# Two splits of the PSUM banks, the decays of a group made ahead, and an eighth tile for sample states

## The chip, the cores and the metric

The kernel runs on one NeuronCore of a Trainium2 chip. The metric is the device time of one execution in microseconds; the time given is the median of several runs. A profile is one execution more, recorded by the hardware profiler, and has a time of its own. The core has five engines that work side by side, each through its own queue of instructions: TensorE (PE; its loading of the stationary operand is shown as PEld), VectorE (DVE), ScalarE (ACT), GpSimd (POOL) and SyncE (SP), which here only issues transfers. TensorE writes to PSUM, eight banks of 128 x 512 fp32 numbers.

## The reference

One inference step of a model with two layers, for a prompt of 256 tokens and eight sample streams of 16 tokens (384 tokens together), width 1024, all in fp32:

```python
for i in range(DEPTH):                       # DEPTH = 2
    h = rms_norm(x, norm_mix[i])
    if i % 2 == 0:                           # layer 0: short conv and attention
        out, k, v, lf, sc = even_mixer(h, ...)
    else:                                    # layer 1: Mamba-2 SSD (SSM)
        out, cs, ss = odd_mixer(h, ...)
    x = x + out
    f, fs = conv_ffn(rms_norm(x, norm_ffn[i]), ...)
    x = x + f
```

`even_mixer` projects to a gated short convolution (512 channels) and to eight attention heads with a forget gate, joins the two and multiplies by `w_out`. `odd_mixer` projects to z, to the convolved x, B and C, and to dt, and runs a state-space scan over 32 heads in four groups:

```python
cum = jnp.cumsum(dtc * a, axis=2)
seg = cum[:, :, :, None] - cum[:, :, None, :]
decay = jnp.exp(jnp.where(tri[:, :, None, None], seg, -jnp.inf))
mix = cb[..., None] * decay * dtc[:, :, None]
y_intra = jnp.einsum('bcqsgr,bcsgrp->bcqgrp', mix, xc)
```

To it comes the part of the state that a sequence brings along (a state of 64 x 128 per head for each sample stream), and the state after the step is an output. `conv_ffn` multiplies by `w_up` (2 x 2816 columns), convolves one half, gates, and multiplies by `w_down`.

## The kernel before

All 384 tokens stand in the free dimension of the tiles, features in the partitions. Weights come as 219 tiles of 128 x 1024 (`raw`), loaded by SP in the order of their use. Each is split into two fp32r tiles, `wh` by ACT (L364) and `wl` by DVE (L365); the activations are split likewise (`Hh`, `Hl`), and a product is three matmuls (`three`, L404): high x high, high x low, low x high (profile lines L405 to L407). `wraw` and `wsp` have three buffers each. `fm_group` makes 128 output features for all tokens in one bank; `tm_group` makes three banks, one for each 128 tokens, with 512 features.

The stages in order of time: q, k and v (`tm_group`, three banks each, to about 78 us); the attention, with the short convolution's projections (`short_conv`: banks gc, gu, gb) beside it; the output projection `op`; the first FFN (`fa`, `fg`, then `fd`, to 470 us); the SSM layer (to about 788 us: `xbc` in `conv4`, z, and `op` in `add_out`); the second FFN.

Engine queues are laid out when the program is built. The framework takes the instructions in the order of the Python program as their priority, and puts on each engine the one of highest priority that can run by its own estimate of durations and with tiles that are free; `tc.high_priority()` moves weights ahead. Where the program calls `fill(n)`, some steps of a generator with projections are put between the steps of the scan. On the chip each queue runs in the order laid out. A pool's `bufs` says how many tiles of a tag exist; an instruction that needs one more waits for a release. Matmul results live in two PSUM pools, opened once for the whole kernel: `mm`, three banks, for the projections (`pmm`), and `aux`, five banks, for all else (`paux`).

In the SSM layer `channels(g)` makes a group's x, B, C (`xt`, `CB`, `Bt`, `Bm`), and `scan` runs over b = 0, 1 (two blocks of 128 prompt tokens) and b = 2 (the samples). In blocks 0 and 1 it makes the decays of eight heads in two halves: `td`/`tdr` on DVE (L1044), a matmul `sg` with cum as both operands (L1047), Relu and Exp on ACT into `dec` (tag `td`, two buffers; L1053, L1054), and `mix` from `dec` and `CB` on DVE (L1055). In block 2 it goes over the eight sample states in two fours (`par`): load `h0` (SP, L1079), matmul `yi` (L1082), matmul `hn` (L1089), a product on POOL and a sum on DVE in place, store `o_hs` from ACT's queue (L1096). The prompt's state after block 1, `S1` (L1110), takes a tile of the same tag `h0`, with seven buffers, and is stored as `o_hp` from POOL's queue (L1113).

Of the kernel before, what the change touches and what calls it, by code (L numbers as in the profile page):

```python
# [18 lines left out]
P = 128  # L19
# [64 lines left out]
def _pack(x):  # L84

    x = {k: np.asarray(v) for k, v in x.items()}
    a = {}
    tok = np.concatenate([x["x_prompt"][0], x["x_sample"].reshape(NB * LB, -1)], 0)
    a["x"] = tok.T.reshape(KT, P, NT)

    blocks = []

    def fm(w, cols, kts=None):

        n = w.shape[0] // P
        for c in cols:
            for kt in (range(n) if kts is None else kts):
                blocks.append(w[kt * P:(kt + 1) * P, c:c + P])

    def tm(w, c):  # L100

        for kt in range(w.shape[0] // P):
            blocks.append(w[kt * P:(kt + 1) * P, c:c + 512])

    wi, wo = x["w_in_even"][0], x["w_out_even"][0]
    tm(wi, 1536), tm(wi, 2048), tm(wi, 2560)
    for i in range(4):
        fm(wi, (512 + P * i, 1024 + P * i, P * i))
    first = [P * m for m in range(3)]
    fm(wo, first, range(0, 4))  # L110
    fm(wo, first, range(4, 8))
    fm(wo, range(3 * P, 1024, P))

    def ffn(layer):
        wu, wd = x["w_up"][layer], x["w_down"][layer]
        for j in range(NF):
            fm(wu, (P * j, P * (NF + j)))
        fm(wd, range(0, 1024, P))

    ffn(0)  # L120
    wi, wo = x["w_in_odd"][0], x["w_out_odd"][0]

    def chan(g):
        fm(wi, (4096 + P * g, 4608 + P * g))
        fm(wi, range(2048 + 512 * g, 2560 + 512 * g, P))

    def out(g):
        for c in (0, 512):
            for kt in range(4 * g, 4 * g + 4):
                blocks.append(wo[kt * P:(kt + 1) * P, c:c + 512])  # L130

    chan(0)
    for g in range(4):
        if g < 3:
            chan(g + 1)
        tm(wi, 512 * g)
        if g:
            out(g - 1)
    out(3)
    ffn(1)  # L140
    w = np.concatenate(blocks, 1)
    a["w"] = w.reshape(P, -1, RC).transpose(1, 0, 2)

    def small(w):

        t = np.zeros((P, KT, 32), np.float32)
        t[:, :, :w.shape[1]] = w.reshape(KT, P, -1).transpose(1, 0, 2)
        return t.reshape(P, -1)

    a["wsm"] = np.concatenate([small(x["w_in_even"][0][:, 3072:]), small(x["w_in_odd"][0][:, 5120:])], 1)  # L150

    prm = np.zeros((P, NPRM), np.float32)

    def put(name, arr, off=0):
        o = COL[name] + off
        prm[:, o:o + arr.shape[1]] = arr

    for l in range(2):
        put("g_mix", _cols(x["norm_mix"][l]), 8 * l)
        put("g_ffn", _cols(x["norm_ffn"][l]), 8 * l)  # L160
        for t in range(3):
            put("cvf", _cols(x["ffn_conv_w"][l, t]), (3 * l + t) * NF)
        put("cvfb", _cols(x["ffn_conv_b"][l]), l * NF)
    for t in range(3):
        put("cva", _cols(x["conv_a_w"][0, t]), 4 * t)
    for t in range(4):
        put("cvs", _cols(x["ssm_conv_w"][0, t]), 24 * t)
    put("sng", _cols(x["ssm_norm"][0]))
    put("cvsb", _cols(x["ssm_conv_b"][0]))
    put("qg", np.tile(x["q_norm"][0], 2)[:, None])  # L170
    put("kg", np.tile(x["k_norm"][0], 2)[:, None])

    def row(v):
        return np.broadcast_to(np.asarray(v)[None, :], (P, len(v)))

    put("bf", row(x["b_forget"][0]))
    put("dtb", row(x["dt_bias"][0]))
    put("alog", row(x["a_log"][0]))
    put("dsk", row(x["d_skip"][0]))
    a["prm"] = prm  # L180
    a["cst"] = _constants()
    a["krow"] = row(np.tile(x["k_norm"][0], 8))

    def state(s, n):

        b, t, f = s.shape
        return s.transpose(2, 0, 1).reshape(n, P, b, t).transpose(1, 0, 2, 3)

    a["st_sc"] = state(x["state_sconv"][0], 4)
    a["st_ssm"] = state(x["state_ssm_conv"][0], 24)  # L190
    a["st_ffn"] = np.stack([state(x["state_ffn_conv"][l], NF) for l in range(2)])
    ck = x["cache_fox_k"][0].reshape(NB, P, 4, P)
    a["kc"] = ck.transpose(0, 3, 2, 1)
    a["vc"] = x["cache_fox_v"][0].reshape(NB, P, 512)
    a["lfc"] = x["cache_fox_logf"][0].transpose(2, 0, 1)
    a["h0"] = x["state_ssm"][0].reshape(NB, 4, 512, P).transpose(0, 1, 3, 2)
    return {k: np.ascontiguousarray(v) for k, v in a.items()}
# [37 lines left out]
def build(nc, tc, d, stop=None):  # L235
# [5 lines left out]
    wsp = ctx.enter_context(tc.tile_pool(name="wsp", bufs=3))  # L241
    tiny = ctx.enter_context(tc.tile_pool(name="tiny", bufs=2))

    mm = ctx.enter_context(tc.tile_pool(name="mm", bufs=3, space=PSUM))
    aux = ctx.enter_context(tc.tile_pool(name="aux", bufs=5, space=PSUM))

    def pmm(name):
        return mm.tile([P, 512], F32, tag="mm", name=name)

    def paux(name):  # L250
        return aux.tile([P, 512], F32, tag="aux", name=name)


    X = cp.tile([P, KT, NT], F32, name="X")
# [156 lines left out]
    def run(gen):  # L411
        while True:
            try:
                next(gen)
            except StopIteration as e:
                return e.value
# [92 lines left out]
        return t[:, 0:w + 256], t[:, w + 256:w + 256 + NB * (LB + w)].rearrange("p (b t) -> p b t", t=LB + w)  # L509

    def finish():
        ctx.close()


# [164 lines left out]
    def beside_attention():  # L679
        for i in range(4):  # L680
            yield from short_conv(i)
        nc.gpsimd.dma_start(out=d["o_sc"], in_=osc)
        for m in range(3):
            ops.append(pmm("op"))
            yield from fm_group(ops[m], yh, yl, range(0, 4), True, False)

# [143 lines left out]
            tt(yl[rows, 4:8, o].rearrange("p k (b t) -> p k b t", t=LB), src, f32(oh), ALU.subtract)  # L830

    fill.rest()
    for m in range(KT):
        if m < 3:
            ps = ops[m]
            run(fm_group(ps, yh, yl, range(4, 8), False, True))
        else:
            ps = pmm("op")
            run(fm_group(ps, yh, yl, range(KT)))
        residual(m, ps)  # L840
        norm_tile(m, "g_ffn", 0, e2)
    r = norm_factor(e2)
    e2s.close()
    ev.close()
# [53 lines left out]


    od = ExitStack()  # L900
    o0 = od.enter_context(tc.tile_pool(name="o0", bufs=1))
    o1 = od.enter_context(tc.tile_pool(name="o1", bufs=2))
    sts = o0.tile([P, 24, NB, 3], F32, name="sts")
# [36 lines left out]
    for b in range(3):  # L940
# [6 lines left out]
    act(ea, prr("alog", 32), AF.Exp)  # L947
    stt(dA.rearrange("p (b h) -> p b h", h=32), dt.rearrange("p (b h) -> p b h", h=32), -1.0,
        ea.unsqueeze(1).broadcast_to([P, 3, 32]), ALU.mult, ALU.mult)
    dAm = t512("h0", 7, (P, NB, 32))  # L950
    tt(dAm, dA[:, 64:96].unsqueeze(1).broadcast_to([P, NB, 32]),
       C("bmask").unsqueeze(2).broadcast_to([P, NB, 32]), ALU.mult)
    ps = paux("E")
# [19 lines left out]
    act(ck[64:96, :, :], cs, AF.Copy, scale=-1.0)  # L973
    V.tensor_scalar_mul(ck[96:128, :, :], f32(cq[32:64, :, :]), -1.0)
    tt(wdt, E[:, 96:192], dt, ALU.mult)
    tjd = t512("h0", 7, (P, 32, LB))
    tt(tjd, dA[:, 64:96].unsqueeze(2).broadcast_to([P, 32, LB]),
       C("Tj").unsqueeze(1).broadcast_to([P, 32, LB]), ALU.mult)
    ps = paux("sgS")
# [39 lines left out]
    def bc64(ap):  # L1019
        return ap.unsqueeze(2).broadcast_to([P, 8, 64])  # L1020

    def scan(fill, after, g, Cg, Cm, CB, Bt, Bm, xt):
        h8 = slice(8 * g, 8 * g + 8)

        def col(t, b, off=0):
# [1 line left out]

        ys, S0 = [], None
        for b in range(3):
            o = slice(b * P, (b + 1) * P)  # L1030
            x3 = heads(xt[:, b, :])
            xdt = t512("xdt")
# [4 lines left out]
            tt(heads(y[:, :]), x3, bc64(prr("dsk", 32)[:, h8]), ALU.mult, G)  # L1037
            mix = t512("mix", 1, (P, 8, P))
            if b < 2:
                sg = []  # L1040
                for hf in range(2):
                    c0 = 8 * g + 4 * hf
                    td = o1.tile([P, 4, P], F32R, tag="tdr", name="tdr", bufs=2)
                    tt(td, f32(cq[:, b, :]).unsqueeze(1).broadcast_to([P, 4, P]),  # L1044
                       C("hsel")[:, c0:c0 + 4].unsqueeze(2).broadcast_to([P, 4, P]), ALU.mult)
                    ps = paux("sg")
                    T.matmul(ps, lhsT=ck[:, b, :], rhs=td.rearrange("p h q -> p (h q)"), start=True, stop=True)  # L1047
                    sg.append(ps)
                fill(2)
                for hf, ps in enumerate(sg):  # L1050
                    dec = t512("td", 2, (P, 4, P))

                    act(dec.rearrange("p h q -> p (h q)"), ps, AF.Relu, scale=-1.0)  # L1053
                    act(dec, dec, AF.Exp, scale=-1.0)  # L1054
                    tt(mix[:, 4 * hf:4 * hf + 4, :], dec, CB[:, b, :].unsqueeze(1).broadcast_to([P, 4, P]), ALU.mult)  # L1055
            else:
                dsv = decS[:, 128 * g:128 * g + 128].rearrange("p (h j) -> p h j", j=LB)
                tt(mix.rearrange("p h (b j) -> p h b j", j=LB),
# [13 lines left out]
            if b == 2:  # L1072

                pi = paux("yi")
                for par in range(2):
                    four = []
                    for i in range(4):
                        h0 = t512("h0", 7)
                        nc.sync.dma_start(out=h0, in_=d["h0"][2 * i + par, g])  # L1079
                        four.append(h0)  # L1080
                    for i in range(4):
# [20 lines left out]
            if b < 2:  # L1102
# [4 lines left out]
                    S0 = t512("S0", 1)  # L1107
                    act(S0, ph, AF.Copy)
                else:
                    S1 = t512("h0", 7)  # L1110
                    tt(heads(S1[:, :]), heads(S0[:, :]), bc64(E[:, 224 + 8 * g:232 + 8 * g]), ALU.mult)
                    tt(S1, S1, ph, ALU.add)
                    nc.gpsimd.dma_start(out=d["o_hp"][g], in_=S1)  # L1113
            ys.append(y)
            after(b, y)
        return ys

    def project_z():
        ps = yield from tm_group("z")
# [61 lines left out]
    def add_out(yh, yl, factor):  # L1181
        for m0 in (0, 4):
            ws = [W.take(512) for _ in range(4)]
            for m in range(4):
# [8 lines left out]
                else:  # L1193
# [2 lines left out]
                    tt(X[:, m0 + m, :], X[:, m0 + m, :], o, ALU.add)  # L1196
                    norm_tile(m0 + m, "g_ffn", 1, o1)

    cur, out = run(channels(0)), None
    for g in range(4):  # L1200
        got = {}
# [7 lines left out]

        fill = Fill(beside_scan(), FILL_O[g])  # L1210
        gate = Gate(fill, got, g == 3)
        scan(fill, gate, g, *cur)
        if "z" not in got:
            fill.rest()
        gate(None, None)
# [28 lines left out]
```

## Time and profile before

| | |
|---|---|
| median of three runs | 1090.59 us (1090.09, 1090.59, 1093.41) |
| profiled execution, its own time | 1091.81 us |
| its span, first to last instruction | 1090.0 us |
| mean granted TensorE clock | 0.987 |
| busy: PE, PEld, DVE, ACT, POOL | 97%, 89%, 68%, 45%, 14% |

Times in the profile are counted from the first instruction. A row of the waits has the waiting engine and line, what it waited for, the sum in us, how often, and the longest. A row of the timeline has start, duration, engine, line, operation, out<-in, shapes, and in brackets how long the engine stood idle before it and what ended that. A row of windows has the stretch, its length, then busy time and instructions of PE, PEld, DVE, ACT and POOL, the granted TensorE clock, the share of the DMA engines and GB/s. A TensorE row lasts longer than the distance to the next one, since matmuls overlap in the pipeline; the pace is read from the starts.

### The profile page before, as it was taken

The page shows a single profiled execution, that of the slowest core. Times are in us where ns is not written, and L with a number is a line of the kernel's source. Part 1 is how long each engine was busy: PE and PEld are TensorE (multiplying, and loading weights), DVE is VectorE, ACT ScalarE, POOL GpSimd, SP SyncE. Part 2 cuts the span into 40 slices and gives each one's busy share as a digit, 9 for nine tenths or more (in the row PEclk, how much of TensorE's full clock was granted, in tenths as well). Part 3 has the DMA queues.
Part 4 walks back from the last instruction along what each step waited for, and adds up shares of the span by engine and source line. Part 5 has one row for each costly group of instructions (what it writes and reads, how often), then busy time and mean ns, then how long its engine had stood idle before and what let it go on. Part 6 is the DMA issues. An engine that isn't in the chain of part 4 may idle for free.

```text
span 1090.0 us, 16757 instructions
## 1 busy us (share of the span) xinstructions
PE 1059.2 (97%) x6332; PEld 972.6 (89%) x6332; DVE 738.8 (68%) x1321; ACT 490.8 (45%) x753; POOL 151.4 (14%) x377
## 2 busy tenths in 40 slices
PE   8979999999999999999899999999999999999998
PEld 6758899999999999999759689785799999999998
DVE  6876666777677734468879768777687767775332
ACT  6334334444444433347738438454354444444221
POOL 0030010100000000004362422323101000000000
PEclk9989999999999999999999999999899999999999
DMA  8432544444434443433445445436334444434441
GB/s 275 127 107 88 175 118 136 122 120 133 122 130 127 132 134 118 136 109 97 135 165 161 144 130 176 155 122 214 102 116 126 132 122 130 129 123 142 139 149 41
DMA packets 47944, 146.07 MB, mean 134 GB/s; under 512 B 5720, under 2 KB 7976, under 8 KB 47864
## 3 DMA queue, kind: packets, MB, share of 16 engines
q1 hardware_dynamic: 41976, 132.55, 39.3%
q10 hardware_dynamic: 4608, 8.39, 2.0%
q0 software_dynamic: 1280, 4.06, 1.1%
q8 instruction: 50, 0.82, 0.3%
q14 instruction: 30, 0.25, 0.1%
HBM read 131.61 MB, written 13.37 MB: 133 GB/s over the span
## 4 chain that ended last, share of the span: by engine, by line
PE 49%; DVE 4%; DMA 2%; issue 1%; ACT 1%; ACTq 0%; DVEq 0%; SPq 0%
PE fg L405 3%; PE fg L406 3%; PE fd L406 3%; PE fd L407 3%; PE fd L405 3%; PE fg L407 3%; PE xbc L405 3%; PE xbc L406 3%; PE xbc L407 3%; PE fa L406 3%; PE fa L407 3%; PE fa L405 3%; PE op L407 2%; PE op L405 2%; PE op L406 2%; PE z L405 2%
## 5 line engine op out<-in xcount | busy, mean ns | idle before, releaser
L280 DVE TENSOR_TENSOR wl<-raw,wh 128x1024 fp32r<-128x1024 f32 (+1 forms) x205 | 252.7, 1234 | 130.6 <-ACT wh L286 129.0
L286 ACT ACTIVATE wh<-raw 128x1024 fp32r<-128x1024 f32 (+1 forms) x205 | 216.2, 1055 | 252.9 <-PE fd L406 95.0
L405 PE MATMUL fg<-Hh,wh 128*128 128x384 f32 x352 | 118.8, 337 | 1.1 <-DVE pad L280 0.8
L405 PE MATMUL fa<-Hh,wh 128*128 128x384 f32 x352 | 118.6, 337 | 0.0
L406 PE MATMUL fa<-Hl,wh 128*128 128x384 f32 x352 | 118.5, 337 | 0.1
L406 PE MATMUL fg<-Hl,wh 128*128 128x384 f32 x352 | 118.4, 336 | 0.0
L407 PE MATMUL fa<-Hh,wl 128*128 128x384 f32 x352 | 118.3, 336 | 0.0
L407 PE MATMUL fg<-Hh,wl 128*128 128x384 f32 x352 | 118.3, 336 | 0.0
L405 PE MATMUL fd<-hh,wh 128*128 128x384 f32 x352 | 118.3, 336 | 0.0
L407 PE MATMUL fd<-hh,wl 128*128 128x384 f32 x352 | 118.3, 336 | 0.0
L406 PE MATMUL fd<-hl,wh 128*128 128x384 f32 x352 | 118.3, 336 | 0.0
L283 DVE SCALAR_TENSOR_TENSOR c<-pad,prm,c 128x400 f32<-128x400 f32 (+1 forms) x160 | 101.7, 643 | 6.7 <-ACT c L286 4.9
L405 PEld LDWEIGHTS fg<-Hh,wh 128*128 128x128 f32 x352 | 66.2, 188 | 1.9 <-ACT R L286 1.1
L406 PEld LDWEIGHTS fa<-Hl,wh 128*128 128x128 f32 x352 | 66.2, 188 | 0.5 <-DVE Hl L283 0.4
L406 PEld LDWEIGHTS fg<-Hl,wh 128*128 128x128 f32 x352 | 66.2, 188 | 0.1
L405 PEld LDWEIGHTS fa<-Hh,wh 128*128 128x128 f32 x352 | 66.2, 188 | 0.1
L407 PEld LDWEIGHTS fg<-Hh,wl 128*128 128x128 f32 x352 | 66.2, 188 | 0.0
L407 PEld LDWEIGHTS fa<-Hh,wl 128*128 128x128 f32 x352 | 66.2, 188 | 0.0
L405 PEld LDWEIGHTS fd<-hh,wh 128*128 128x128 f32 x352 | 66.2, 188 | 0.0
L406 PEld LDWEIGHTS fd<-hl,wh 128*128 128x128 f32 x352 | 66.2, 188 | 0.0
L407 PEld LDWEIGHTS fd<-hh,wl 128*128 128x128 f32 x352 | 66.2, 188 | 0.0
L405 PE MATMUL xbc<-Hh,wh 128*128 128x384 f32 x192 | 66.0, 344 | 0.0
(808 smaller groups left out, 2145.0 us busy)
## 6 DMA issues: line engine op xcount, KB each, us to landing
raw<-w SPq DMA_DIRECT2D x219, 512.0 KB, 3.5
kc<-kc SPq DMA_DIRECT2D x8, 256.0 KB, 4.0
vc<-vc SPq DMA_DIRECT2D x8, 256.0 KB, 3.8
X<-x SPq DMA_DIRECT2D x8, 192.0 KB, 4.6
o_y<-X SPq DMA_DIRECT2D x8, 192.0 KB, 2.5
o_k<-kraw POOLq DMA_DIRECT2D x3, 256.0 KB, 2.5
o_v<-vt POOLq DMA_DIRECT2D x3, 256.0 KB, 4.3
cst<-cst SPq DMA_DIRECT2D x1, 617.0 KB, 6.1
```

The lines of the kernel that those rows point to most:

```text
L280: (eng or V).tensor_tensor(out=out, in0=a, in1=b, op=op)
L283: V.scalar_tensor_tensor(out=out, in0=a, scalar=s, in1=b, op0=op0, op1=op1)
L286: S.activation(out, a, f, **kw)
L405: T.matmul(out, lhsT=ah, rhs=bh, start=start, stop=False)
L406: T.matmul(out, lhsT=ah, rhs=bl, start=False, stop=False)
L407: T.matmul(out, lhsT=al, rhs=bh, start=False, stop=stop)
```

## The change

It has four parts. The PSUM pools are opened as `mm` with four banks and `aux` with four, and closed and opened again with three and five at the SSM layer. The output projection of layer 0 goes in two fours of tiles: the first halves of four tiles (the four k-tiles of the short convolution), then their second halves (attention); the weights are packed in that order. The decays of both prompt blocks of a group are made in one piece, `decays(g)`: four products, four matmuls, four Relu, then four Exp, with four buffers of the tag `td`; group 0's ahead of its channels, group g+1's at the start of block 2 of group g, where `fill(4)` stands in place of the `fill(2)` of blocks 0 and 1. The tag `h0` has eight buffers.

```diff
-    mm = ctx.enter_context(tc.tile_pool(name="mm", bufs=3, space=PSUM))
-    aux = ctx.enter_context(tc.tile_pool(name="aux", bufs=5, space=PSUM))
+    def share(n, name):
+        if psum:
+            psum["stack"].close()
+        st = psum["stack"] = ExitStack()
+        psum["mm"] = st.enter_context(tc.tile_pool(name="mm" + name, bufs=n, space=PSUM))
+        psum["aux"] = st.enter_context(tc.tile_pool(name="aux" + name, bufs=8 - n, space=PSUM))
+    share(4, "0")
...
-        for m in range(3):
+        for m in range(4):
             ops.append(pmm("op"))
             yield from fm_group(ops[m], yh, yl, range(0, 4), True, False)
...
-    for m in range(KT):
-        if m < 3:
-            ps = ops[m]
-            run(fm_group(ps, yh, yl, range(4, 8), False, True))
-        else:
-            ps = pmm("op")
-            run(fm_group(ps, yh, yl, range(KT)))
-        residual(m, ps)
-        norm_tile(m, "g_ffn", 0, e2)
+    for m0 in (0, 4):
+        ps = ops if m0 == 0 else [pmm("op") for _ in range(4)]
+        for m in range(4):
+            if m0:
+                run(fm_group(ps[m], yh, yl, range(0, 4), True, False))
+        for m in range(4):
+            run(fm_group(ps[m], yh, yl, range(4, 8), False, True))
+            residual(m0 + m, ps[m])
+            norm_tile(m0 + m, "g_ffn", 0, e2)
...
     od = ExitStack()
+    share(3, "1")
...
+    def decays(g):
+        sg, out = [], []
+        for b in range(2):
+            for hf in range(2):
+                c0 = 8 * g + 4 * hf
+                td = o1.tile([P, 4, P], F32R, tag="tdr", name="tdr", bufs=2)
+                tt(td, f32(cq[:, b, :]).unsqueeze(1).broadcast_to([P, 4, P]),
+                   C("hsel")[:, c0:c0 + 4].unsqueeze(2).broadcast_to([P, 4, P]), ALU.mult)
+                ps = paux("sg")
+                T.matmul(ps, lhsT=ck[:, b, :], rhs=td.rearrange("p h q -> p (h q)"), start=True, stop=True)
+                dec = t512("td", 4, (P, 4, P))
+                act(dec.rearrange("p h q -> p (h q)"), ps, AF.Relu, scale=-1.0)
+                out.append(dec)
+        for dec in out:
+            act(dec, dec, AF.Exp, scale=-1.0)
+        return out[0:2], out[2:4]
...
         for b in range(3):
+            if b == 2 and g < 3:
+                decs = decays(g + 1)
+                fill(4)
...
-                fill(2)
-                for hf, ps in enumerate(sg):
-                    dec = t512("td", 2, (P, 4, P))
-                    act(dec.rearrange("p h q -> p (h q)"), ps, AF.Relu, scale=-1.0)
-                    act(dec, dec, AF.Exp, scale=-1.0)
-                    tt(mix[:, 4 * hf:4 * hf + 4, :], dec, CB[:, b, :].unsqueeze(1).broadcast_to([P, 4, P]), ALU.mult)
+                for hf in range(2):
+                    tt(mix[:, 4 * hf:4 * hf + 4, :], decs[b][hf], CB[:, b, :].unsqueeze(1).broadcast_to([P, 4, P]),
+                       ALU.mult)
...
-                        h0 = t512("h0", 7)
+                        h0 = t512("h0", 8)
...
+    decs = decays(0)
     cur, out = run(channels(0)), None
...
-        scan(fill, gate, g, *cur)
+        decs = scan(fill, gate, g, decs, *cur)
```

More of the change, by code (lines that the diff above doesn't have):

```diff
@@ L108, in _pack @@
         fm(wi, (512 + P * i, 1024 + P * i, P * i))
[L109 to L112, printed above, removed]
+    for m0 in (0, 4):
+        mts = [P * m for m in range(m0, m0 + 4)]
+        fm(wo, mts, range(0, 4))
+        fm(wo, mts, range(4, 8))
     def ffn(layer):
@@ L242, in build @@
     tiny = ctx.enter_context(tc.tile_pool(name="tiny", bufs=2))
-    mm = ctx.enter_context(tc.tile_pool(name="mm", bufs=3, space=PSUM))
-    aux = ctx.enter_context(tc.tile_pool(name="aux", bufs=5, space=PSUM))
+    psum = {}
+    def share(n, name):
[5 more added lines that the diff above has]
+    share(4, "0")
     def pmm(name):
-        return mm.tile([P, 512], F32, tag="mm", name=name)
+        return psum["mm"].tile([P, 512], F32, tag="mm", name=name)
     def paux(name):
-        return aux.tile([P, 512], F32, tag="aux", name=name)
+        return psum["aux"].tile([P, 512], F32, tag="aux", name=name)
     X = cp.tile([P, KT, NT], F32, name="X")
@@ L511, in finish @@
     def finish():
+        psum["stack"].close()
         ctx.close()
@@ L832, in build @@
     fill.rest()
-    for m in range(KT):
-        if m < 3:
-            ps = ops[m]
-            run(fm_group(ps, yh, yl, range(4, 8), False, True))
-        else:
-            ps = pmm("op")
-            run(fm_group(ps, yh, yl, range(KT)))
-        residual(m, ps)
-        norm_tile(m, "g_ffn", 0, e2)
+    for m0 in (0, 4):
+        ps = ops if m0 == 0 else [pmm("op") for _ in range(4)]
[6 more added lines that the diff above has]
+            norm_tile(m0 + m, "g_ffn", 0, e2)
     r = norm_factor(e2)
@@ L949, in build @@
         ea.unsqueeze(1).broadcast_to([P, 3, 32]), ALU.mult, ALU.mult)
-    dAm = t512("h0", 7, (P, NB, 32))
+    dAm = t512("h0", 8, (P, NB, 32))
     tt(dAm, dA[:, 64:96].unsqueeze(1).broadcast_to([P, NB, 32]),
@@ L975, in build @@
     tt(wdt, E[:, 96:192], dt, ALU.mult)
-    tjd = t512("h0", 7, (P, 32, LB))
+    tjd = t512("h0", 8, (P, 32, LB))
     tt(tjd, dA[:, 64:96].unsqueeze(2).broadcast_to([P, 32, LB]),
@@ L1020, in bc64, with scan @@
         return ap.unsqueeze(2).broadcast_to([P, 8, 64])
-    def scan(fill, after, g, Cg, Cm, CB, Bt, Bm, xt):
+    def decays(g):
[14 more added lines that the diff above has]
+        return out[0:2], out[2:4]
+    def scan(fill, after, g, decs, Cg, Cm, CB, Bt, Bm, xt):
         h8 = slice(8 * g, 8 * g + 8)
@@ L1039, in scan @@
             if b < 2:
-                sg = []
                 for hf in range(2):
[L1042 to L1048, printed above, removed]
-                fill(2)
-                for hf, ps in enumerate(sg):
-                    dec = t512("td", 2, (P, 4, P))
-                    act(dec.rearrange("p h q -> p (h q)"), ps, AF.Relu, scale=-1.0)
-                    act(dec, dec, AF.Exp, scale=-1.0)
-                    tt(mix[:, 4 * hf:4 * hf + 4, :], dec, CB[:, b, :].unsqueeze(1).broadcast_to([P, 4, P]), ALU.mult)
+                    tt(mix[:, 4 * hf:4 * hf + 4, :], decs[b][hf], CB[:, b, :].unsqueeze(1).broadcast_to([P, 4, P]),
+                       ALU.mult)
             else:
@@ L1109, in scan @@
                 else:
-                    S1 = t512("h0", 7)
+                    S1 = t512("h0", 8)
                     tt(heads(S1[:, :]), heads(S0[:, :]), bc64(E[:, 224 + 8 * g:232 + 8 * g]), ALU.mult)
@@ L1115, in scan @@
             after(b, y)
-        return ys
+        return decs
     def project_z():
```

## The prediction

> **What bounds the kernel now.** I read the page first, then the waits of TensorE, then windows around the longest of them, then the timeline at each place that the change touches.
>
> ```profile
> span 1090.0 us, 16757 instructions
> ...
> PE 1059.2 (97%) x6332; PEld 972.6 (89%) x6332; DVE 738.8 (68%) x1321; ACT 490.8 (45%) x753; POOL 151.4 (14%) x377
> ...
> PE 49%; DVE 4%; DMA 2%; issue 1%; ACT 1%; ACTq 0%; DVEq 0%; SPq 0%
> ```
>
> TensorE works for 97% of the span and holds by far the largest share of the chain that ended last. The change takes no matmul away, so it can save no more than TensorE's 1090.0 - 1059.2 = 30.8 us of idle time, and what a lowered clock adds to the busy time. The waits of TensorE say which idle time that is (in total, times, longest):
>
> ```profile
> PE v L405 <- DVE kraw L565: 3.9, 1, 3.9
> PE y L1065 <- DVE mix__4942 L280: 3.2, 1, 3.2
> PE yi L1082 <- DMA h__7516<-h: 3.0, 1, 3.0
> ...
> PE s L713 <- POOL cpad L658: 2.0, 1, 2.0
> PE yi L1082 <- DMA h__6151<-h: 1.9, 1, 1.9
> ...
> PE yi L1082 <- DMA h__5464<-h: 1.1, 1, 1.1
> PE v L406 <- DVE wl L280: 1.1, 1, 1.1
> ...
> PE fg L405 <- DVE pad L280: 0.8, 1, 0.8
> ```
>
> Six of these lie where the change works: the two of v (PSUM banks before the SSM layer), the one of mix (decays), the three of h (tiles for sample states). Behind the long ones the clock drops. The windows show the stretch, TensorE's busy time and count, and after POOL the granted clock:
>
> ```profile
> 58.60:65.50 6.90, 4.18 (x10) 3.31 (x11) 6.39 (x21) 0.60 (x1) 0.00 (x0) 0.51 0.04 14
> 230.00:478.00 248.00, 248.00 (x1433) 247.75 (x1432) 150.63 (x243) 101.08 (x130) 11.26 (x69) 1.00 0.41 127
> 523.00:526.40 3.40, 3.40 (x9) 2.17 (x8) 1.85 (x5) 3.36 (x5) 1.68 (x4) 0.51 0.00 0
> 628.70:632.10 3.40, 3.40 (x9) 2.66 (x9) 1.89 (x3) 1.34 (x2) 0.70 (x1) 0.51 0.00 0
> 765.20:772.00 6.80, 6.80 (x18) 4.71 (x20) 3.30 (x5) 0.47 (x2) 1.04 (x1) 0.51 0.43 116
> ```
>
> The row 230:478 is the undisturbed case: full clock, no idle time, 248.00/1433 = 173 ns from one matmul to the next. The others follow the waits of v, mix, h__6151 and h__7516 at half clock. Such a stretch costs its busy time x 0.49: 2.05, 1.67, 1.67 and 3.33 us.
>
> **Eight tiles for sample states.** A group reads eight states and writes S1 in a tile of the same tag, so nine tiles pass through seven places. The timeline of group 3:
>
> ```profile
> 749.50 0.58 POOL L1113 DMA_DIRECT2D o_hp<-h__7382  x1
> ...
> 753.75 0.33 SPq L1079 DMA_DIRECT2D h__7514<-h  x1
> ...
> 760.71 1.28 ACT L286 ACT_TABLE_LOAD   x1 [5.65 <-DVE h__7434 L280]
> ...
> 761.12 0.33 SPq L1079 DMA_DIRECT2D h__7516<-h  x1
> ...
> 764.37 1.04 PE L1082 MATMUL yi<-h__7516,Cm 128*32 128x512 f32 x2 [3.04 <-DMA h__7516<-h]
> ```
>
> The seventh load goes out when S1's store has landed (753.75), the eighth only when the group's first state has been stored (761.12). With one place more the seventh goes early and the eighth takes the moment of the seventh, 7.4 us sooner here, against a wait of 3.0. On SP's queue no load of weights then stands behind a load that waits for o_hs; one still stands behind the wait for o_hp, as now. Saved: 1.1 + 1.9 + 3.0 = 6.0 us of waits and 1.67 + 3.33 = 5.0 of clock: **-11.0**. Late next is POOL's and DVE's work on the states, for which z's and op's matmuls are cover, as now.
>
> **Four banks for the projections, before the SSM layer.** The group v needs three banks; with three in all, it gets them as the copies of k come.
>
> ```profile
> 49.36 0.69 DVE L565 COPY kraw<-k 128x512 f32<-128x512 f32 x1 [0.37 <-ACT hsq L286]
> ...
> 51.71 0.39 PE L405 MATMUL v<-wh,Hh 128*128 128x512 f32 x1
> ...
> 60.58 0.69 DVE L565 COPY kraw<-k 128x512 f32<-128x512 f32 x1
> ...
> 61.32 0.79 PE L405 MATMUL v<-wh,Hh 128*128 128x512 f32 x1 [3.93 <-DVE kraw L565]
> ...
> 65.90 0.39 PE L407 MATMUL v<-wh,Hl 128*128 128x512 f32 x1
> ...
> 69.40 0.39 PE L407 MATMUL v<-wh,Hl 128*128 128x512 f32 x1
> ```
>
> From 51.71 only the first of v's three banks is free; TensorE runs ahead in it until the three pairs of weight tiles (wsp, three buffers, two k-slices each) are held, and stands until k's second copy, which DVE reaches at 60.58. With a fourth bank k's first group need not wait for q, v finds one bank idle and takes k's first at 50.05, so two of v's groups can run. Six k-slices x two groups x three products are 36 matmuls of 233 ns (the last two rows: 15 steps in 3.50 us) = 8.4 us, up to 60.1. Remaining: 61.32 - 60.1 = 1.2 us. Of 3.9 + 1.1 = 5.0 us thus 3.8 go; 1.2 is shorter than the shortest gap here that lowered the clock (1.9), so 2.05 goes too: **-5.9** (bounds -7.05 and 0).
>
> The other pool shrinks from five banks to four. In the attention po, two s and two pt are then too many by one, and a pt waits for an s to be read. Its cover is short_conv:
>
> ```profile
> 132.28 0.60 PE L822 MATMUL aoT<-cst,ao 128*128 128x128 f32 x4
> ...
> 159.60 0.34 PE L405 MATMUL gb<-Hh,wh 128*128 128x384 f32 x1
> ```
>
> Its matmuls go on for 27 us after the attention's last transposes. So a longer attention costs 0, and only what exceeds the 27 us otherwise. The wait at s (2.0) I leave as it is.
>
> **The output projection in fours.** The same 192 matmuls; four first halves instead of three go ahead of the attention's results, into dense work, so nothing is gained. New is that the last four tiles finish 12 x 173 ns = 2.1 us apart instead of 4.2, so residual and norm crowd at the start of the FFN. FFN 1 begins behind such half groups today and waits 0.8 us for pad with three banks; with four it has a bank in hand. 0 to +0.8, taken 0.
>
> **The change of pools at the SSM layer.** A pool opened on the place of a closed one waits for all of its tiles:
>
> ```profile
> 470.15 0.34 PE L405 MATMUL xbc<-Hh,wh 128*128 128x384 f32 x1
> 470.35 0.55 DVE L280 TENSOR_TENSOR X<-X,fd 128x384 f32<-128x384 f32 x1 [1.97 <-PE fd L407]
> ...
> 479.57 0.49 ACT L286 ACTIVATE R<-Rp 128x384 f32<-128x384 f32 x1 [3.18 <-PE Rp L498]
> ...
> 480.11 0.55 POOL L905 DMA_DIRECT2D sts<-st_ssm  x1 [103.66 <-ACT R L286]
> ```
>
> (sts reads only HBM, and still goes when the FFN's tiles are done.) The new mm lies on old mm banks alone, so xbc starts after fd's last residual, 470.90, instead of 470.15: **+0.8**. The new aux waits for R (480.06), and dt's matmuls, which use it, with it; xbc is their cover.
>
> **Decays a group ahead.** Each group's 4 products tdr, 4 matmuls, 4 Relu and 4 Exp stay, but go as one piece ahead of block 2 of the group before (group 0's ahead of its projections).
>
> ```profile
> 514.29 0.59 ACT L286 ACTIVATE td__4966<-sg 128x512 f32<-128x512 f32 x1
> ...
> 517.15 0.63 ACT L286 ACTIVATE td__4966<-td__4966 128x512 f32<-128x512 f32 x1
> ...
> 518.78 0.34 PE L405 MATMUL xbc<-Hh,wh 128*128 128x384 f32 x1
> ...
> 521.60 0.68 DVE L280 TENSOR_TENSOR mix__4942<-td__4966,CB__4714 128x512 f32<-128x512 f32 x1
> ...
> 522.34 0.69 PE L1065 MATMUL y<-xdt__4936,mix__4942 128*64 128x64 f32 x16 [3.22 <-DVE mix__4942 L280]
> ```
>
> Today mix comes at the end of TensorE, Relu, a table load, Exp and then a place on DVE. The first tdr ran much earlier:
>
> ```profile
> L280 DVE TENSOR_TENSOR tdr<-cq,cst x16: 676/683/1212, 505.5 to 739.6; 128x512 fp32r<-128x512 f32 x16
> ```
>
> After the change all four decays of the group can follow on that, 16 us ahead of today's mix, and mix needs only them and CB. TensorE has xbc until its wait begins at 522.34 - 3.22 = 519.1. Of DVE's work, two or three tdr (0.68 each) come to lie ahead of mix, which fits. **-4.9** (3.2 and 1.67 of clock; bounds -4.9 and 0). Exp then runs in one stretch of a group, so there are fewer table loads (1.28 each, above); ACT is 45% busy, so that saves no time by itself.
>
> The new cost is the piece on ACT: 4 x 0.59 + 1.28 + 4 x 0.63 + 1.28 = 7.4 us in which its queue makes no weights. A weight tile lasts TensorE 24 x 173 ns = 4.2 us. With only one in hand, each of three pieces could cost 3.2 us and 1.67 of clock, 14.6 together; with two in hand, nothing. The nearest row is ACT's 5.65 us behind h__7434 above, under which TensorE did not wait for weights, so I take 0. On DVE the four tdr (4 x 0.683 = 2.7 us) precede block 2's mix; fill(4) and z are cover, and without it they would cost 2.7 a group.
>
> The program's order is laid out anew everywhere, with waits that no row shows. Bounds: the smaller waits of the scans go too (-2), or the piece above costs 14.6. I take +2, the size of the wait at s, an order that fits badly today.
>
> **Sum:** -11.0 - 5.9 - 4.9 + 0.8 + 2 = -19.0 us. The profiled execution took 1091.81 for its span of 1090.0, 1.2 above the median of 1090.59; less 19 it would be 1072.8, and the median 1071.6, said as **1072**.
>
> [...]
>
> **Rivals.**
> 1. The waits move: the new order brings others at v and mix, and only the states pay: -11.0 + 0.8 = 1080. For it: DVE was 6.39 of 6.90 us busy around v, so that it may be the true limit there. Against it: short_conv can fill.
> 2. Both new pools wait for both old ones. xbc then waits for R: 480.1 - 470.3 = 9.8 us, and up to 6.8 us at half clock, 3.3: 1072 + 12 = 1084. Against it: the banks do not overlap.
> 3. Slower: the decays' piece starves TensorE of weights. If no finished tile is in hand, three pieces cost 7.4 + 1.67 each, 27 us: 1099. It decides from 6.3 us a piece. For it: ACT's queue stood behind one store for 5.65 us. [...]
> 4. The eighth tile is not used as meant: another early tile of the tag takes it and the last load still follows the first store: 1072 + 11 = 1083.
> [...]
>
> **Chances.** Forecast (1064 to 1078) 0.55; rival 1 0.17; 2 0.08; 3 0.08; 4 0.07; 5 0.05. The range 1064 to 1088 takes in all but rival 3 and the tails. A measurement here tells 0.3%, 3.3 us: faster is below 1087.3. Rival 3 and a little more is slower, 0.10; the upper ends of 1, 2 and 4 give 0.08 for the same; faster 0.82.
>
> **What would show it.** Right: no TensorE wait on a DMA h, all eight loads out before the first o_hs; v's wait near 1; no wait on mix in group 0; fewer table loads; a gap of 0.8 at the first xbc; four half-clock stretches fewer. Wrong: new waits on wh or wl at block 2, on sg's tdr, or xbc starting after R.

## The result, and the profile after

The changed kernel takes 1079.05 us (median; 1077.92 to 1080.92) where the kernel before, run beside it again, takes 1092.0. The ratio is 0.9881, with a 95% interval from 0.985 to 0.9911: 13.0 us less, between 16.4 and 9.7. A second set of runs of the same kernel (below) gave 0.989 [0.9859, 0.992]. The forecast was 1072, with a range of 1064 to 1088. The direction is right, and about a third of the expected 19 us is missing. The profiled execution took 1079.71.

The page of the kernel after, its head and its chain:

```profile
span 1077.9 us, 16678 instructions
...
PE 1054.0 (98%) x6332; PEld 972.6 (90%) x6332; DVE 739.3 (69%) x1321; ACT 476.5 (44%) x741; POOL 158.2 (15%) x377
...
PE 45%; DVE 8%; ACT 2%; issue 1%; DMA 1%; ACTq 0%; DVEq 0%; POOL 0%
```

TensorE's idle time went from 30.8 to 1077.9 - 1054.0 = 23.9 us, and its busy time, of the same 6332 matmuls, from 1059.2 to 1054.0. So 6.9 us of the gain are idle time and 5.2 are busy time. The half clock explains 1.6 of the 5.2: TensorE was busy at half clock for 24.7 us before and for 21.5 after, and half of the difference counts. What the other 3.6 are, the two traces do not say. DVE's share of the chain doubled, from 4% to 8%.

TensorE's waits after (in total, times, longest):

```profile
PE y L1084 <- DVE mix__5075 L288: 3.2, 2, 2.5
PE yT L596 <- DVE h__7491 L288: 2.5, 1, 2.5
PE kT L596 <- DVE kraw L288: 2.2, 1, 2.2
PE yT L596 <- DVE yi__7567 L288: 1.4, 1, 1.4
PE sg L1042 <- DVE tdr L288: 1.3, 2, 0.7
...
PE xbc L413 <- DVE X L288: 0.7, 1, 0.7
...
PE op L413 <- ACT zs__7506 L294: 0.6, 1, 0.6
```

All three waits on a DMA h are gone, both on v are gone, and the one of 2.0 on s. The wait on mix is still there, in another block, and there are new ones: on tdr, and three at the end of group 3 (yi, h, zs). Four stretches at half clock are left, 23.8 us in all; before there were five, 27.2 us in all. The windows of the kernel after (stretch, busy time of PE, PEld, DVE, ACT, POOL, then the clock):

```profile
66.80:70.20 3.40, 3.40 (x15) 3.33 (x14) 2.44 (x2) 2.48 (x4) 3.40 (x2) 0.50 0.28 113
517.40:524.20 6.80, 6.18 (x40) 5.88 (x36) 4.28 (x10) 1.36 (x4) 2.13 (x7) 0.50 0.86 308
613.00:619.80 6.80, 6.78 (x13) 3.31 (x11) 2.80 (x5) 0.00 (x0) 1.15 (x1) 0.50 0.73 231
756.30:763.10 6.80, 5.00 (x20) 4.91 (x21) 4.66 (x10) 1.87 (x7) 0.00 (x0) 0.50 0.64 208
```

Three of the four lie in the SSM layer and last 20.4 us, where that layer had 13.6 before. The states' waits are gone, but the clock now falls at other places.

**The states' loads** in group 3 are as forecast:

```profile
735.44 0.38 SPq L1098 DMA_DIRECT2D h__7495<-h  x1
740.65 0.33 SPq L1098 DMA_DIRECT2D h__7497<-h  x1
...
748.92 0.34 ACTq L1115 DMA_DIRECT2D o_hs<-h__7430  x1
```

Seven go early, the eighth at 740.65, 8.3 us ahead of the first store o_hs. Rival 4 falls.

**Group 0** shows what became of the wait on mix. The timeline of the kernel after, DVE, POOL and TensorE:

```profile
506.43 1.22 DVE L288 TENSOR_TENSOR wl<-raw,wh 128x1024 fp32r<-128x1024 f32 x1
...
511.88 1.42 DVE L291 SCALAR_TENSOR_TENSOR c<-pad,prm,c 128x408 f32<-128x408 f32 x1
513.23 2.06 DVE L288 TENSOR_TENSOR wl<-raw,wh 128x1024 fp32r<-128x1024 f32 x1
...
516.66 1.52 DVE L288 TENSOR_TENSOR mix__5075<-td__4648,CB__4750 128x512 f32<-128x512 f32 x1
518.11 0.63 DVE L291 SCALAR_TENSOR_TENSOR c<-pad,prm,c 128x408 f32<-128x408 f32 x1
...
512.83 1.38 POOL L288 TENSOR_TENSOR y__5073<-xt__4764,prm 128x512 f32<-128x512 f32 x1
514.17 2.02 POOL L288 TENSOR_TENSOR y__5267<-xt__4764,prm 128x512 f32<-128x512 f32 x1
...
516.89 0.74 PE L1084 MATMUL y<-xdt__5069,mix__5075 128*64 128x64 f32 x16 [2.53 <-DVE mix__5075 L288]
```

The decays (td) are long finished. What is late is DVE: mix stands behind c and wl, and while POOL works on its five products (xw and y, 509.9 to 517.7) the same c takes 1.42 us instead of 0.63 and wl 2.06 instead of 1.22. Against what they take elsewhere in this trace, xdt (1.53), c, wl and the two halves of mix (0.93 and 1.52) lose 3.6 us here, an estimate that is near the 3.2 us of waiting. The kernel before has the same slow rows (c 1.42 at 516.32, wl 2.06 at 517.67). What is new is that block 1's y, at 539.39 before, now comes at 516.89, in the middle of this.

### The profile page after: what moved, and what is told of

Same layout as the page of the kernel before. It is cut to its first block, busy times and chain, and to the rows that moved or that the text cites. A ratio compares the mean times of both kernels' runs of the same rounds, so it can differ in the third digit from the quotient of the medians.

```text
span 1077.9 us, 16678 instructions
## 1 busy us (share of the span) xinstructions
PE 1054.0 (98%) x6332; PEld 972.6 (90%) x6332; DVE 739.3 (69%) x1321; ACT 476.5 (44%) x741; POOL 158.2 (15%) x377
## 4 chain that ended last, share of the span: by engine, by line
PE 45%; DVE 8%; ACT 2%; issue 1%; DMA 1%; ACTq 0%; DVEq 0%; POOL 0%
PE fg L413 3%; PE fg L414 3%; PE fd L414 3%; PE fd L415 3%; PE fd L413 3%; PE fg L415 3%; PE fa L415 3%; PE fa L414 3%; PE fa L413 3%; DVE c L291 2%; PE z L413 2%; PE xbc L414 2%; PE z L414 2%; PE xbc L415 2%; PE xbc L413 2%; PE z L415 2%
## 5 line engine op out<-in xcount | busy, mean ns | idle before, releaser
L414 PE MATMUL xbc<-Hl,wh 128*128 128x384 f32 x192 | 66.7, 347 | 0.0
L415 PE MATMUL xbc<-Hh,wl 128*128 128x384 f32 x192 | 66.3, 345 | 0.0
```

The costliest lines, as they stand in the source:

```text
L414: T.matmul(out, lhsT=ah, rhs=bl, start=False, stop=False)
L415: T.matmul(out, lhsT=al, rhs=bh, start=False, stop=stop)
```

## The experiments

Each time is compared with runs of the kernel before on the same chip; a ratio is turned into us with their median, 1090.3 to 1090.8.

### The parts one by one: banks, states, decays

**e1, banks alone**: the kernel before with the diff's parts for `share`, the weights' order and the output projection, and nothing else.

```diff
+    share(4, "0")
...
+    share(3, "1")
     o0 = od.enter_context(tc.tile_pool(name="o0", bufs=1))
```

> The kernel before with the bank part alone: four and four banks up to the SSM layer, three and five from there, the output projection in fours; seven tiles for states and the old decays. Theory T (the two traces: the even layer gave 11.8 us, because k starts in the fourth bank while q still waits for its last input, and the SSM layer gave almost nothing): about -11 us, TensorE's first k near 21.7, last row of q without a wait of 2.2, first xbc 0.7 late; from there on the trace of before. Rival P (the prediction's sizes): -5.9 + 0.8 = -5.1 us. If the even layer's gain needs the other parts, it is between.

Measured: 1081.69 us, ratio 0.9928 [0.9911, 0.9944], **-7.9** us (-9.7 to -6.1). Between the two theories. The waits of TensorE that it has left:

```profile
PE y L1075 <- DVE mix__4950 L288: 3.4, 1, 3.4
PE yi L1092 <- DMA h__7524<-h: 2.9, 1, 2.9
PE kT L596 <- DVE kraw L288: 2.2, 1, 2.2
```

v and s are gone from the list, and the wait on kT has grown from 0.7 to 2.2. By the waits -3.9 - 1.1 - 2.0 + 1.5, by the clock -2.05 (58.7 to 65.5) and +0.7 at the first xbc: -6.9. The 12 us by which the FFN starts earlier in its trace are more than that, because the profiled run of before had one more stretch of half clock, at 24.6 to 31.4, 3.3 us worth. The traces of e2 and e3 below, with the same code up to there, do not have it. So my theory T, which gave that stretch to the fourth bank, is wrong in size.

**e2, states alone**:

```diff
-                        h0 = t512("h0", 7)
+                        h0 = t512("h0", 8)
```

(and the same number at the tag's three other tiles).

> The kernel before with eight instead of seven tiles for sample states and nothing else. Rival P (the prediction): the three waits on h (6.0 us) and two stretches of half clock (5.0) go: -11 us. Theory T (in the SSM layer DVE and the banks of the other pool set the pace, and the loads were only what came last): the waits on h go, but others of 1 to 2 us take their place and the half-clock stretches come at other places: -1 to -5 us. Rival D: the states alone pay 11 and the decays took it back in the change; then this run gives -11 and the decays alone +5 to +10.

Measured: 1081.16 us, 0.9919 [0.9906, 0.9931], **-8.8** us (-10.3 to -7.5). No wait on h is left, and one of 2.2 on yT took the place of group 3's:

```profile
PE yT L587 <- DVE y__7305 L280: 2.2, 1, 2.2
```

That is nearer to the prediction's -11 than to the -1 to -5 that T expected. So the states do pay by themselves, and something takes it back in the full change.

**e3, decays alone**: the diff's parts for `decays` and `scan`, without the rest.

```diff
+            if b == 2 and g < 3:
+                decs = decays(g + 1)
+                fill(4)
...
+    decs = decays(0)
     cur, out = run(channels(0)), None
```

> The kernel before with the decays made in one piece a group ahead (four tiles for them), and nothing else: three and five banks throughout, seven tiles for states. Rival P: the wait on mix of 3.2 and its stretch of half clock go: -4.9 us. Theory T: group 0's wait on mix moves to the next block, since y now comes earlier than DVE can make mix; 0 to -2 us. Rival D (the decays' piece costs DVE and ACT time at block 2 or leaves TensorE without cover): +5 to +10 us.

Measured: 1089.61 us, 0.999 [0.9979, 1.0002], **-1.1** us (-2.3 to +0.2). Not the -4.9, and not the +5 to +10 of rival D either. Its longest wait is new:

```profile
PE yi L1091 <- DMA h__7489<-h: 5.4, 1, 5.4
```

With seven tiles the last state's load now comes later still against TensorE's order.

**e5, banks and states** (the kernel after with the old decays and the old scan):

```diff
-            if b == 2 and g < 3:
-                decs = decays(g + 1)
-                fill(4)
...
+                fill(2)
+                for hf, ps in enumerate(sg):
+                    dec = t512("td", 2, (P, 4, P))
```

> The kernel after with its decays part undone: banks and eight tiles for states, decays as before. The single parts measured -7.9 (banks), -8.8 (states) and -1.1 us (decays) against the kernel before. Theory T2 (the decays part and the states part do not add up: the decays part takes back in the scans what the states part gives): about -17 us, 1073.5, faster than the kernel after by 3 to 5. Rival (the parts add and the kernel after was measured low by chance of the clock): -16.7 here too, but then the kernel after, run again beside it, is at -17.8 and no slower than this one. Rival 2 (banks and states do not add): no better than -13.

Measured: 1070.54 us, 0.9807 [0.9777, 0.9837], **-21.0** us (-24.3 to -17.8). Its page:

```profile
span 1069.7 us, 16700 instructions
...
PE 1049.0 (98%) x6332; PEld 967.7 (90%) x6332; DVE 737.0 (69%) x1321; ACT 489.2 (46%) x751; POOL 152.8 (14%) x377
```

**e6, the kernel after again**, on the same chip as e5:

> The kernel after, unchanged, so that the other kernels of this call can be set against it on the same chip. Its first time was 13 us below the kernel before, with an interval from -16.4 to -9.7. If the parts add up, it is at -17.8; under theory T2 it stays near -13.

Measured: 1078.66 us, 0.989 [0.9859, 0.992], **-12.0** us. The runs of e5 (1069.28 to 1071.43) and of e6 (1078.02 to 1080.56) do not overlap. So theory T2 holds: with the decays part the kernel is 8.1 us slower than without it. Banks and states together gave all that was forecast for the whole, and a little more than their sum by single runs (16.7), within the intervals.

### What in the decays part costs it: the fill

The decays part moves TensorE's filling work: the two units that stood ahead of mix in each of blocks 0 and 1 are dropped, and four come behind the decays at block 2. Three kernels undo one half or both.

**e4**, the two units put back, the four kept:

```diff
             if b < 2:
+                fill(2)
                 for hf in range(2):
```

> The kernel after, with the two units of TensorE filling work that stood ahead of mix in blocks 0 and 1 put back there. Theory T (y comes too early: group 0's block 1 waits 3.2 us in all for mix with 6.8 us of half clock, as DVE was busy 11.9 of 12.4 us before; and xT falls between hn's matmuls and takes the bank that the fourth hn needs): about 3 us of waits and one or two stretches of half clock fewer, -3 to -8 us against the kernel after, 1071 to 1076. Rival: the waits are set by DVE's total work in the layer, so more fill early only moves them to z and the states, 0 to +4 against the kernel after.

**e7**, the two put back and the four taken out, so that the fill stands as before:

```diff
                 decs = decays(g + 1)
-                fill(4)
...
             if b < 2:
+                fill(2)
                 for hf in range(2):
```

> The kernel after with the decays made a group ahead, but TensorE's filling work where it was before: two units ahead of mix in blocks 0 and 1, none at block 2 after the decays. The scans then use as much filling work as before the change. Theory T2a (what the decays part takes back comes from moving the fill: y comes 20 us early where DVE is not ready, and xT falls among the states' matmuls): the wait on mix goes, the fill does not run out, and the kernel is at -17 to -22 against before. Rival T2b (the cost is the decays' piece itself, four products on DVE and 7.4 us on ACT at one place): no better than the kernel after, -13 or less, with waits behind the piece at block 2.

**e9**, only the four taken out:

```diff
                 decs = decays(g + 1)
-                fill(4)
```

> The kernel after without the four units of filling work behind the decays at block 2, and without the two units ahead of mix that it had dropped: the one half of the fill's move undone. The kernel with both halves undone was at -21, the kernel after at -12. Theory Y (the cost is y coming too early, ahead of DVE): little is regained, -11 to -15 against before, with the waits on mix and xT. Rival F (the cost is the fill at block 2, which draws xT's and z's groups in among the states): most is regained, -17 to -21.

Measured, against the kernel before:

| | no fill at block 2 | four units at block 2 |
|---|---|---|
| no fill ahead of mix | e9: 1081.21, 0.9907 [0.9881, 0.9933], -10.1 | after: 1078.66, -12.0 |
| two units ahead of mix | e7: 1069.82, 0.9804 [0.9774, 0.9834], -21.4 | e4: 1085.41, 0.9951 [0.9934, 0.9969], -5.3 |

e7 regains the 9 us; T2a's forecast holds, and the decays' piece itself (T2b) costs nothing there. It gains nothing either: e5, with the old decays, is at -21.0 on the same chip. e9 regains nothing, as theory Y had it. e4 I had wrong: it is slower than the kernel after, by more than either forecast allowed. Its waits say why:

```profile
PE yT L596 <- ACT y__5645 L294: 4.8, 1, 4.8
PE yT L596 <- ACT y__6458 L294: 4.8, 1, 4.8
```

The fill of a group is a fixed stock (the next group's channels, z, the last group's op). What is used up early is missing at the group's end, where yT waits for the scaled y. And without the two units ahead of mix, TensorE comes to block 1 of group 0 ahead of DVE (the first row), and later groups have waits on xT and yT. In e9:

```profile
PE y L1083 <- DVE mix__5075 L288: 3.1, 2, 2.5
PE xT L1025 <- ACT sq__5976 L294: 2.6, 1, 2.6
PE yT L596 <- DVE h__7491 L288: 2.5, 1, 2.5
```

How much of the 8 to 9 us is waiting, and how much clock, the page of e7 tells:

```profile
span 1069.8 us, 16667 instructions
...
PE 1048.0 (98%) x6332; PEld 969.1 (91%) x6332; DVE 739.0 (69%) x1321; ACT 476.0 (44%) x741; POOL 158.8 (15%) x377
```

From e7 to the kernel after, idle time rises from 21.8 to 23.9, by 2.1, and busy time from 1048.0 to 1054.0, by 6.0. TensorE was busy at half clock for 10.2 us in e7 and for 21.5 in the kernel after; half of the difference is 5.6. So about two thirds of the 8.1 us between these two traces is clock (with e6's trace, 4.0 of 6.4).

Where the loss lies, the starts of TensorE's first y in each group tell. These are the stretches from one to the next, in us, with the half clock in them in brackets:

| from the first y of | e7 | the kernel after | e6, the same kernel |
|---|---|---|---|
| group 0 to that of group 1 | 63.5 (3.4) | 65.4 (6.8) | 65.2 (6.8) |
| group 1 to that of group 2 | 67.8 (0) | 70.8 (6.8) | 70.7 (6.8) |
| group 2 to that of group 3 | 75.5 (0) | 77.7 (0) | 77.8 (0) |
| group 3 to the end of the layer's last op | 69.3 (3.4) | 71.4 (6.8) | 71.3 (6.8) |

(That end is at 787.8 in e7 and at 795.9 in the kernel after; in the kernel before it is at 808, not at the 788 that stands ahead of the prediction.) Group 0, where the kernel after waits 3.2 us for mix, makes only 1.8 of the 9.2 us, since e7 stands as long at the same place, as the next section shows. The rest lies in groups 1 to 3, where no wait on mix is longer than 0.4. There the kernel after has a wait of 0.9 on xT with 6.8 us of half clock behind it in group 1, 0.7 on tdr in each of groups 1 and 2, and 2.5 and 1.4 on yT in group 3, where e7 has 1.7 and 1.1. So it is shown that the move of the fill costs the 8 to 9 us. That it costs them because TensorE runs ahead of DVE holds for group 0 alone; what the fill covered in the other groups stays open.

### Why group 0 still waits: DVE beside POOL

In e7 the wait on mix is gone and one on cb of 3.2 stands at the same place, with DVE busy for 10.97 of the 11.50 us ahead of it:

```profile
520.28 0.94 PE L1001 MATMUL cb<-C__4980,B__4979 128*128 128x128 f32 x6 [3.22 <-ACT C__4980 L294]
```

**e11** takes e7 and makes the product of x with the skip weights on DVE:

```diff
-            tt(heads(y[:, :]), x3, bc64(prr("dsk", 32)[:, h8]), ALU.mult, G)
             mix = t512("mix", 1, (P, 8, P))
...
+            tt(heads(y[:, :]), x3, bc64(prr("dsk", 32)[:, h8]), ALU.mult)
             py = paux("y")
```

> The kernel with the decays ahead and the fill where it was (-21 against before), and besides the product of x with the skip weights (y) on DVE, after mix, instead of on POOL. Theory C (in group 0 DVE is the limit because its products run at half pace beside POOL's: c 1.42 us instead of 0.64, wl 2.06 instead of 1.23 in the traces): each product costs DVE 0.69 and gives back 0.8 or more, POOL's first product for S comes no later, and the wait of 3.2 us in group 0 (cb on C) shrinks by 1 to 3 us with its half-clock stretch: -22 to -26 against before. Rival: DVE's queue only gets 12 more products of 0.69 us, and group 3's end, where DVE is also late, waits longer: -17 to -20.

Measured: 1069.17 us, 0.9807 [0.9784, 0.9831], -21.0. No change against e7 that these intervals can tell. In the trace DVE has more to do (744.9 us busy where e7 has 739.0), and is done earlier.

```profile
512.87 1.21 DVE L288 TENSOR_TENSOR wl<-raw,wh 128x1024 fp32r<-128x1024 f32 x1
...
515.95 0.63 DVE L291 SCALAR_TENSOR_TENSOR c<-pad,prm,c 128x408 f32<-128x408 f32 x1
...
518.24 0.94 PE L1001 MATMUL cb<-C__4979,B__4978 128*128 128x128 f32 x6 [0.21 <-ACT C__4979 L294]
```

The wait of 3.22 is 0.21, and group 0 has no half clock. But xT now waits 2.3 at 544, and the end of group 3 has 6.8 us of half clock where e7 has 3.4. From group 0's first y to group 1's, e11 takes 2.5 us less than e7; from group 3's to the layer's end it takes 1.1 more. So DVE's slow products are the likely cause of e7's wait in group 0, though the edit changed the order of DVE's queue as well. The kernel after itself was not run with this product on DVE.

**e12** adds to e11 that group 3's stores of states go out on POOL's queue, four at a time:

```diff
-                        nc.scalar.dma_start(out=d["o_hs"][bb, g], in_=h0)
+                        if g < 3:
+                            nc.scalar.dma_start(out=d["o_hs"][bb, g], in_=h0)
+                    if g == 3:
+                        for i in range(4):
+                            nc.gpsimd.dma_start(out=d["o_hs"][2 * i + par, g], in_=four[i])
```

> The last kernel (decays ahead, fill as before, skip product on DVE; -21 against before) and besides group 3's stores of sample states issued by POOL after each four, instead of by ACT one by one. Theory Q (in group 3's end z's Silu stands 5.7 us behind the stores on ACT's queue, and TensorE then 1.1 us for zs and 2.8 us for yT): the wait on zs goes and the second four of states comes earlier; 2 to 4 us less, 1065 to 1068. Rival: yT waits for banks that DVE frees with the states' adds, so only the 1.1 us goes and POOL's products of the second four come later behind the stores: within 2 us of the last kernel, 1068 to 1071.

Measured: 1067.89 us, 0.9788 [0.9763, 0.9813], **-23.1**. The wait on zs is gone, and those on yT stay:

```profile
PE yT L596 <- DVE h__7520 L288: 1.7, 1, 1.7
...
PE yT L596 <- DVE h__7518 L288: 1.2, 1, 1.2
```

By the time, both theory Q (1065 to 1068) and the rival (within 2 us of e11) can stand; by the waits it is the rival: yT needs a bank that DVE frees with the states' adds. This kernel has the lowest median of all, 11 us below the kernel after, though e5, e7, e11 and e12 can't be told apart by their intervals.

### Two tries at the fourth bank that missed

To see k's start alone, **e8** was to hold the fourth bank until q's copies, by a transpose into a tile `hold` ahead of q; **e10** by a matmul of cumP.

```diff
+    hold = pmm("hold")
+    T.matmul(hold[:, :256], lhsT=f32(cumP[:, 0:P]), rhs=f32(cumP[:, :]), start=True, stop=True)
-    q = qk("q")
+    q = qk("q", hold)
...
+        if hold is not None:
+            V.tensor_copy(hr, hold[:, 0:8])
```

> The kernel after with the fourth bank of the projections held by another tile until q's copies are made, so that k can't start in it; v has it. It adds one transpose ahead of q and a copy of 8 columns. Theory T (most of the even layer's gain is k starting beside q's last wait for input): k starts near 29 as before, and 3 to 6 us of the kernel after's gain are lost. Rival P (the prediction: the gain is at v alone): v's waits stay gone and no more than 1 us is lost.

> The kernel after with the fourth bank held until q's copies are made, now written by a matmul of zeros that needs no loaded input (the earlier try read a table that lands late, and TensorE stood 15.6 us at the start). k can't start in the fourth bank; v has it. Theory T (most of the even layer's gain is k starting beside q's last wait for input and its copies): k starts 5 to 7 us later than in the kernel after, near 26 to 29, and 3 to 6 us are lost, about 1083. Rival P (the gain is at v alone): no more than 1 us is lost, 1079 to 1080.

Measured: e8 1094.52 (1.0033 [1.0016, 1.0049]) and e10 1110.1 (1.0179 [1.0158, 1.02]). Neither tells what it should. The matmul of e10 was meant to need no loaded input, but it reads cumP, for which TensorE waits 4.5 us. q, which came at 5.8 us, now starts at 22.9 and 42.5, since in TensorE's order `hold` and all that stands ahead of it in the program then precede q. In e10:

```profile
PE ss L492 <- DVE acc L288: 15.3, 1, 15.3
PE hold L635 <- DVE cumP L288: 4.5, 1, 4.5
```

What k's early start is worth by itself stays open.

## Why the prediction was right and wrong

- **States, -11.0: right, and alone a little less.** Alone -8.8 (-10.3 to -7.5); on top of the banks 11.2 by the medians of e1 and e5 (1081.7 - 1070.5) and 13.1 by their ratios. The 6.0 us of waits went as said. Of the 10.2 us of half clock in groups 1 and 3, 3.4 stayed in e2 and in e5, behind the new wait on yT.
- **Banks, -5.9, and pools, +0.8: right in mechanism, too small.** Together -5.1, measured -7.9 (-9.7 to -6.1). The residue of 1.2 at v never came, and the wait of 2.0 on s, which I left, went as well: short_conv now has banks and gc runs at 63.4 instead of 82.8, ahead of s. Against it, kT waits 1.5 longer. The price of the pools was right, and rival 2 fell: xbc waits for X, not for R.

```profile
459.16 0.41 PE L413 MATMUL xbc<-Hh,wh 128*128 128x384 f32 x1 [0.74 <-DVE X L288]
```

- **Out-projection, 0: right.** The first FFN starts without a wait.
- **Decays, -4.9, and the order, +2: wrong; these are the steps that failed.** Alone -1.1, in the change +8.1. The wait of block 0 went as forecast: its mix is done by 500.9. But the -4.9 took it that nothing waits next. In the kernel after, block 1's y comes 22.5 us earlier than before and waits 3.2 for its mix; in e7, with the fill as before, cb waits 3.2 at the same place. I counted DVE's products at 0.68 us and left out that beside POOL's they take longer (in the kernel after xdt 1.53 and a half of mix 1.52), and that DVE was full (there, busy for 11.87 of the 12.40 us from 505.0 to 517.4). And I had written of the four tdr that "fill(4) and z are cover", as if fill(4) were more work. It is the same stock, taken from ahead of mix, and the move costs 8.8 us (e6 less e7, on the same chip). The +2 for the new order, "the size of the wait at s", should have been some 8; how the move costs that much in groups 1 to 3 stays open. The sign that I had named for this, a wait on sg's tdr, came, with 1.3 in all. The forecast with 8 in place of these two terms, -11.0 - 5.9 + 0.8 + 8, is -8, against -12 to -13 measured, and the banks' larger gain (2.8) is over half of what remains.
- **The range held in part by luck.** States, banks and pools gave 21 us where 16.1 were forecast, and the decays part took 8 back where it was to give 2.9. The two errors offset each other in part.
- **ACT's piece, 0: right.** No wait on wh or wl at block 2; e7 has the same piece and is no slower than e5. Rival 3 fell.
- **Rival 1** gave 1080, next to the result, but that is luck: it let only the states pay, while it is the banks and states that pay and the scans that give back.

## What to carry to other kernels

A queue of filling work is a stock. Here moving its draws cost 8 to 9 us and gave nothing; so when a fill moves, price the place that it leaves as well as the place that it goes to. Make the parts of a change one by one: here one part of three cost 8 us of the 21 that the others gave, and the sum looked like a plain success. A single profiled run can carry stretches of half clock that another run of the same kernel lacks (3.4 us at 66.8 in the kernel after, none there in e6); compare two traces by waits first, and by clock only over several runs.

## What the runs showed of the hardware

**The clock changed in steps of 3.41 us.** In the traces of the kernel before and the kernel after, every change of the granted clock up to the last matmuls lies a whole multiple of 3.41 us from every other of the same trace. Half clock (0.50) begins at 24.59, 58.73, 522.94, 628.75 and 765.28 before, at 66.83, 517.39, 612.96 and 756.32 after, and lasts 3.4 or 6.8 us. The starts that were read in e5 (512.7, 755.0), e7 (67.8, 521.8, 753.9) and e9 (516.9, 609.1) lie 71, 133, 68 and 27 such steps apart. The windows ahead of the kernel after's four drops:

```profile
63.40:66.80 3.40, 1.18 (x9) 0.84 (x8) 3.18 (x10) 1.42 (x3) 1.01 (x3) 1.00 0.69 195
514.00:517.40 3.40, 0.87 (x19) 0.58 (x17) 3.40 (x4) 0.00 (x0) 3.40 (x3) 1.00 0.30 82
609.60:613.00 3.40, 2.46 (x10) 0.93 (x9) 2.30 (x3) 2.33 (x5) 3.12 (x5) 0.99 0.00 0
752.90:756.30 3.40, 1.29 (x9) 0.27 (x9) 3.37 (x5) 2.36 (x6) 2.63 (x2) 1.00 0.44 169
```

In three of them TensorE was busy for 0.26 to 0.38 of the time, in the one of 609.6 for 0.72. Ahead of the five drops of the kernel before it was busy for 0.18 to 0.46 of such a window. Of the windows on these steps in the two traces that kept full clock and had no drop behind them, none was busy for less than 0.62 (79.2 in the kernel before). In e7 the windows ahead of the drops at 521.8 and 753.9 were busy for 1.52 and 1.53 of 3.40 us, and one with 2.06 (515.0) had no drop behind it. So ten of these eleven drops follow a window that was busy for less than half of its time. No run tried this by itself.

The same wait can have half clock behind it or not. The kernel after and e6 are one kernel, and both wait 2.2 us for kT; the first has 3.4 us of half clock behind it, the second none (mean clock 0.989 and 0.990). That this goes by where the wait falls on the steps is my reading, and not shown. Runs of one kernel differ by about as much as their clock: the eight of e4 go from 1081.33 us at a mean clock of 0.992 to 1087.89 at 0.986, and 0.006 of 1084 us is 6.5, about the whole difference.

**A drop behind a busier window.** The window of 609.6, busy for 0.72, holds `hn`:

```profile
609.38 0.40 PE L415 MATMUL z<-wh,Hl 128*128 128x512 f32 x1
610.71 0.44 PE L1025 MATMUL xT<-cst,sq__6027 128*128 128x128 f32 x2 [0.94 <-ACT sq__6027 L294]
611.08 1.13 PE L1108 MATMUL hn<-xw__5967,Bm__5134 32*128 32x512 f32 x4
612.14 0.33 PE L1025 MATMUL xT<-cst,sq__6027 128*128 128x128 f32 x1
```

Against it, a window of the kernel after with `hn` and only 0.64 busy (544.7 to 548.1) kept its clock. The ends of matmuls are modelled in the trace, and no run tried this by itself; why the clock fell here stays open.

**DVE beside POOL.** In the kernel after, three of the products c<-pad,prm,c (128x408) lie fully beside a two-tensor product of POOL and take 1.42 us (median), and 64 lie beside none and take 0.64. DVE's sums that read a PSUM bank (X<-X,op) take 0.55 in both cases, two of them fully beside. In group 0 of e11, with fewer of POOL's products, c at 515.95 takes 0.63 and wl at 512.87 takes 1.21.
